# Down-projection by seven block products for nine pairs of feature tiles, in a one-core decoder block

## The chip, the cores and the metric

One core of a Trainium2 chip runs the whole kernel. The metric is device time in microseconds (us). Before the change three runs took 1463.87 us in the median (1459.05 to 1466.71). The engines are TensorE (PE, with its weight loads as PEld), VectorE (DVE), ScalarE (ACT), GpSimd (POOL) and SyncE (SP, which here issues the DMAs).

## The reference, cut to what matters

```python
# L = 1040 positions (16 meta tokens + 1024), D_MODEL = 1024, D_FF = 2816, float32
def _conv_ffn(xn, w_up, conv_w, conv_b, w_down):
    h = xn @ w_up                                      # L x 1024 times 1024 x 5632
    hp = jnp.pad(h, ((0, 0), (CONV_WIDTH - 1, 0), (0, 0)))
    hc = conv_b + sum(conv_w[k] * hp[:, k:k + L] for k in range(CONV_WIDTH))
    gate, up = jnp.split(hc, 2, axis=-1)
    return (jax.nn.silu(gate) * up) @ w_down           # the down-projection: L x 2816 times 2816 x 1024

def reference(...):
    h = concat(meta_tokens, x)
    h = h + _token_mixer(_rmsnorm(h, g_attn), ...)     # two kinds of attention, one output projection
    h = h + _conv_ffn(_rmsnorm(h, g_ffn), ...)
    return _rmsnorm(h, g_final)[:, N_META:]
```

## The kernel before, in words

The kernel runs through attention, the output projection, the up-projection with convolution and gate (the "up phase"), and the down-projection with the last norm (the "down phase"). Every float32 product is made of three matmuls on float32r parts: a matrix is split into a high part (an ACT cast, L856) and a low part (a subtraction, L857, on POOL), and high x high, high x low and low x high are summed in PSUM.

**Up phase (the loop over `ff` from `PLAIN` = 3 to 21, matmuls at L1012).** The 2816 features are 22 tiles of 128. For each feature tile the gate and the up weights (`raw` tiles, two buffers) come in by DMA; POOL makes four sums of their halves (L990 to L993, in `load_up`); four weight entries are split into `dh`/`dl` (three buffers), and seven products of half size give gate and up for both halves of the tokens. These are already Winograd's seven products, on tokens by model dimension. `rest()` ends a tile: `gate` (L1020 to L1024) applies SiLU, multiplies gate and up (L1022) and writes 256 KB of gated features into the DRAM tensor `gated`. `rest()` of one tile is called after the first product of the next tile. The first three feature tiles are done by `plain_chunk`, ahead of this loop. The tokens' own parts `yh`/`yl` and their sums `s1`, `s2`, `s4` stay in SBUF through the phase.

**Down phase (L1077 on).** `load_down` brings in the gated rows of one feature tile (`hr`, 128 features x 1024 tokens) and its rows of `w_down` (`raw`, 128 x 1024), and splits both (L856 on ACT, L857 on POOL, 1024 columns each). Feature tiles go in groups of two, then five times four. For each group, each of eight token tiles and each of two column halves, one PSUM bank takes 3 matmuls of 128x128 by 128x512 per feature tile (L1115), and DVE adds the bank to the residual in SBUF (L1116). In the last group the last norm follows each token tile and its rows go out.

**What sets the order.** The source gives data flow. The framework orders each engine's instructions, DMA issues included, at build time by a simulated timeline, with program order as priority, and an instruction that the simulation finds ready may be put ahead of earlier ones. On the chip each engine then works strictly in that order. All the DMAs here go through SP's one queue. A tile waits until the last reader of what lay at its place is done (`reuse_waits="tile"`). The tiles of the down phase's pool `ph` lie where `yh`, `yl` and, above these, the pool of `s1`, `s2`, `s4` lay.

Of the kernel before, what the change touches and what calls it, by code (L numbers as in the profile page):

```python
# [8 lines left out]
F32 = mybir.dt.float32  # L9
F32R = mybir.dt.float32r  # L10
BF16 = mybir.dt.bfloat16
I32 = mybir.dt.int32
AF = mybir.ActivationFunctionType
ALU = mybir.AluOpType
# [3 lines left out]
P = 128  # L18
D = 1024
SEQ = 1024  # L20
META = 16
L = SEQ + META
KT = D // P
NT = SEQ // P
# [12 lines left out]
HALF = SEQ // 2  # L37
SUB = HALF // 2
PLAIN = 3
G_DOWN = 4  # L40
SLOTS = 9
B_EARLY = 0
TL = True
A_BUFS = 7
# [19 lines left out]
def f(ap):  # L64
    return ap.bitcast(F32)
# [25 lines left out]
def hybrid_block(ctx: ExitStack, tc: tile.TileContext, x, meta, g_attn, w_in, lq1, lk1, lq2, lk2,  # L91
# [49 lines left out]
    def rstd(pool, ss, n, tag):  # L141

        w = pool.tile([P, 4], F32, tag=tag, name=tag, bufs=4)
        l, y, m, u = (w[:n, i : i + 1] for i in range(4))
        nc.scalar.activation(l, ss, AF.Ln, bias=eps[:n], scale=1.0 / D)
        nc.scalar.activation(y, l, AF.Exp, scale=-0.5)
        nc.vector.tensor_scalar(m, ss, 1.0 / D, EPS, op0=ALU.mult, op1=ALU.add)
        nc.vector.tensor_scalar(u, m, y, y, op0=ALU.mult, op1=ALU.mult)
        nc.vector.tensor_scalar(u, u, -0.5, 1.5, op0=ALU.mult, op1=ALU.add)
        nc.vector.tensor_scalar(m, u, y, None, op0=ALU.mult)  # L150
        return m
# [34 lines left out]

    merged = dram.tile([UNITS, P, 2, NQ], F32, name="merged")
    y_rows = dram.tile([NT + 1, P, D], F32, name="y_rows")
    gated = dram.tile([NF, P, SEQ], F32, name="gated")

    left, left_out, right, right_a, right_b = (ExitStack() for _ in range(5))
    pw = ctx.enter_context(tc.tile_pool(name="pw", bufs=1, side="left"))
# [455 lines left out]
    def load_raw(src):  # L648
        raw = pw.tile([P, D], F32, tag="raw", name="raw", bufs=2)
        nc.sync.dma_start(raw, src)  # L650
        return raw
# [13 lines left out]
    def resid(t):  # L665
        return room["accm"][:2] if t == 0 else room["acc"][:, t - 1, :]
# [158 lines left out]


    right_f, right_g, left_s = ExitStack(), ExitStack(), ExitStack()
    pf = right_f.enter_context(tc.tile_pool(name="pf", bufs=1, side="right", reuse_waits="tile"))

    yh = [pf.tile([P, KT, HALF + 2], F32R, name=f"yh{h}") for h in range(2)]  # L830
    yl = [pf.tile([P, KT, HALF + 2], F32R, name=f"yl{h}") for h in range(2)]
    pd = right_f.enter_context(tc.tile_pool(name="pd", bufs=1, side="right", reuse_waits="tile"))
    pg = right_g.enter_context(tc.tile_pool(name="pg", bufs=1, side="right", reuse_waits="tile"))
    gb = pg.tile([P, D], F32, tag="gb", name="g_ffn_b")
    nc.sync.dma_start(gb, g_ffn.broadcast_to([P, D]))
# [16 lines left out]
    def split_w(pool, tags, src, bufs):  # L852
        hi = pool.tile([P, D], F32R, tag=tags[0], name=tags[0], bufs=bufs)
        lo = pool.tile([P, D], F32R, tag=tags[1], name=tags[1], bufs=bufs)
        w = src.shape[-1]
        nc.scalar.copy(hi[:, :w], src)  # L856
        nc.gpsimd.tensor_tensor(lo[:, :w], src, f(hi)[:, :w], op=ALU.subtract)  # L857
        return hi, lo

    def conv(c, src, fc):  # L860

        n = c.shape[-1]
        taps = [src[:, j : j + n] if len(src.shape) == 2 else src[:, :, j : j + n] for j in range(3)]
        nc.scalar.activation(c, taps[2], AF.Identity, bias=cb[:, fc : fc + 1], scale=cw[:, fc, 2:3])
        for j in (1, 0):
            nc.vector.scalar_tensor_tensor(c, taps[j], cw[:, fc, j : j + 1], c, op0=ALU.mult, op1=ALU.add)  # L866
# [132 lines left out]
    def prepare(k):  # L999
        if k < len(entries):  # L1000
            ff, i = entries[k]
            if i == 0:
                load_up(ff)
            ready[k] = split_w(pd, ("dh", "dl"), raws[ff][i], 3)
# [15 lines left out]
    def gate(ff, cg, cu, h):  # L1020
        silu = nc.scalar.activation(cg[:, h], cg[:, h], AF.Silu)
        nc.vector.tensor_tensor(cg[:, h], cg[:, h], cu[:, h], op=ALU.mult)  # L1022
        nc.sync.dma_start(gated[ff, :, HALF * h : HALF * h + HALF], cg[:, h].rearrange("p s c -> p (s c)"))
        return silu  # L1024

    prepare(0)
    prepare(1)
    rest = None
    for ff in range(PLAIN, NF):
        k = 4 * (ff - PLAIN)  # L1030
        cg = pw.tile([P, 2, 2, SUB], F32, tag="wh", name="cg", bufs=2)
        cu = pw.tile([P, 2, 2, SUB], F32, tag="wl", name="cu", bufs=2)
        prepare(k + 2)
        w = ready.pop(k)
        x, y = pair(), pair()
        product(x, w, 0, a11, True, False)
        p1, copied = kept(x, pn, "mc", 2)
        if rest:
            with tc.issue_after(copied.ins):
                rest()  # L1040
        product(y, w, HD, a12, True, True)
        nc.vector.tensor_tensor(y, p1, y, op=ALU.add)
        prepare(k + 3)
        w = ready.pop(k + 1)
        z = pair()
        product(x, w, 0, s2, False, False)
        u2, copied = kept(x, pn, "mc", 2)
        with tc.issue_after(copied.ins):
            conv(cg[:, 0], y, ff)
        product(z, w, HD, s3, True, False)  # L1050
        p7, _ = kept(z, pn, "yb", 1)
        prepare(k + 4)
        w = ready.pop(k + 2)
        product(x, w, 0, s1, False, True)
        u4, copied = kept(x, pn, "mc", 2)
        nc.vector.tensor_tensor(x, p7, x, op=ALU.add)
        product(z, w, HD, a22, False, True)
        nc.vector.tensor_tensor(z, u2, z, op=ALU.add)
        conv(cu[:, 1], x, NF + ff)
        conv(cg[:, 1], z, ff)  # L1060
        prepare(k + 5)
        w = ready.pop(k + 3)
        v = pair()
        product(v, w, 0, s4, True, True)
        nc.vector.tensor_tensor(v, u4, v, op=ALU.add)

        def rest(ff=ff, cg=cg, cu=cu, v=v):
            last = gate(ff, cg, cu, 1)
            conv(cu[:, 0], v, NF + ff)
            return last, gate(ff, cg, cu, 0)  # L1070
    silus = rest()
    banks.close()
    left_s.close()
    right_f.close()
# [1 line left out]

    psd = banks.enter_context(tc.tile_pool(name="psd", bufs=1, space=PSUM, reuse_waits="tile"))  # L1077
    ph = ctx.enter_context(tc.tile_pool(name="ph", bufs=1, side="right", reuse_waits="tile"))
    slot = [0]

    def load_down(ff):
        k = slot[0] % SLOTS
        slot[0] += 1
        hr = pw.tile([P, D], F32, tag="wh", name="hr", bufs=2)
        nc.sync.dma_start(hr, gated[ff])
        got = []
        for what, src in (("h", hr), ("w", load_raw(w_down[P * ff : P * (ff + 1), :]))):
            got.append(split_w(ph, (f"{what}h{k}", f"{what}l{k}"), src, 1))
        return got

    groups, ff = [], 0
    for n in [2] * (NF % G_DOWN // 2) + [G_DOWN] * (NF // G_DOWN):
        groups.append(range(ff, ff + n))
        ff += n
    assert ff == NF
    loaded = {0: [load_down(ff) for ff in groups[0]]}
    with tc.issue_after(silus[0].ins), tc.issue_after(silus[1].ins):
        nc.scalar.preload_act_table_set("natural_log_exp_and_others")
    for gi, group in enumerate(groups):
        last = gi == len(groups) - 1  # L1100
        if last:
            gb = pw.tile([P, D], F32, tag="wl", name="g_final_b", bufs=2)
            nc.sync.dma_start(gb, g_final.broadcast_to([P, D]))
        else:
            loaded[gi + 1] = [load_down(ff) for ff in groups[gi + 1]]
        pairs = loaded.pop(gi)
        for t in range(1, NT + 1):
            h = resid(t)
            tsl = slice(P * (t - 1), P * t)
            for half in range(2):  # L1110
                hs = slice(512 * half, 512 * half + 512)
                ps = psd.tile([P, 512], F32, tag="d", name="ps_d", bufs=8)
                for j, ((gh, gl), (wh, wl)) in enumerate(pairs):
                    for i, (a, b) in enumerate(((gh, wh), (gh, wl), (gl, wh))):
                        nc.tensor.matmul(ps, a[:, tsl], b[:, hs], start=(j == 0 and i == 0), stop=(j == len(pairs) - 1 and i == 2))  # L1115
                nc.vector.tensor_tensor(h[:, hs], h[:, hs], ps, op=ALU.add)  # L1116
            if last:
                ss = pn.tile([P, 1], F32, tag="ssf", name="ssf", bufs=4)
                yn = pw.tile([P, D], F32, tag="wh", name="yn", bufs=2)
                nc.scalar.activation(yn, h, AF.Square, accum_out=ss)  # L1120
                r = rstd(pn, ss, P, "rf")
                for half in range(2):
                    hs = slice(512 * half, 512 * half + 512)
                    nc.vector.scalar_tensor_tensor(h[:, hs], h[:, hs], r, gb[:, hs], op0=ALU.mult, op1=ALU.mult)
                    nc.sync.dma_start(out[P * (t - 1) : P * t, hs], h[:, hs])


# [39 lines left out]
```

## Time and profile before

| | before |
|---|---|
| median of 3 runs | 1463.87 us |
| profiled execution | 1460.51 us, its span 1458.8 us |
| mean granted TensorE clock | 0.979 |
| PE busy | 1379.6 us (95%) |
| DVE / ACT / POOL busy | 854.9 / 687.4 / 679.5 us |
| up phase, L1012, from the chain | 849.99 to 1199.55 us |
| down phase, L1115, from the chain | 1211.06 to 1450.97 us |

The profile is one execution. Its span runs from the first to the last instruction; 1.7 us of the execution's time lie around it. Busy time of an engine is not progress: an instruction that waits inside the engine counts as busy. The chain of waits goes back from the last instruction to whatever released it, so it tells which engine set the end at each time.

### The profile page before, as it was taken

The page shows a single profiled execution, that of the slowest core. Times are in us where ns is not written, and L with a number is a line of the kernel's source. Part 1 is how long each engine was busy: PE and PEld are TensorE (multiplying, and loading weights), DVE is VectorE, ACT ScalarE, POOL GpSimd, SP SyncE. Part 2 cuts the span into 40 slices and gives each one's busy share as a digit, 9 for nine tenths or more (in the row PEclk, how much of TensorE's full clock was granted, in tenths as well). Part 3 has the DMA queues.
Part 4 walks back from the last instruction along what each step waited for, and adds up shares of the span by engine and source line. Part 5 has one row for each costly group of instructions (what it writes and reads, how often), then busy time and mean ns, then how long its engine had stood idle before and what let it go on. Part 6 is the DMA issues. An engine that isn't in the chain of part 4 may idle for free.

```text
span 1458.8 us, 24218 instructions
## 1 busy us (share of the span) xinstructions
PE 1379.6 (95%) x9108; PEld 1275.5 (87%) x9108; DVE 854.9 (59%) x1705; ACT 687.4 (47%) x1379; POOL 679.5 (47%) x706
## 2 busy tenths in 40 slices
PE   5999999998999979898999899999999998999997
PEld 5999999998888877676799899999999997888886
DVE  8377777767676748865777445444454445222235
ACT  6355655665665746433444344444445445212102
POOL 5112222257585655742003466766667649555300
PEclk9999999999999989899999999999999999999999
DMA  5112212212111145345443222222222236433002
GB/s 210 51 33 62 66 52 66 62 47 68 44 51 39 36 123 142 90 96 115 119 158 130 64 84 87 66 80 74 87 85 69 80 102 214 132 115 116 29 15 101
DMA packets 71532, 126.20 MB, mean 87 GB/s; under 512 B 9180, under 2 KB 43612, under 8 KB 71416
## 3 DMA queue, kind: packets, MB, share of 16 engines
q1 hardware_dynamic: 71416, 124.66, 28.0%
q8 instruction: 72, 1.18, 0.3%
q14 instruction: 44, 0.36, 0.1%
HBM read 87.89 MB, written 28.34 MB: 80 GB/s over the span
## 4 chain that ended last, share of the span: by engine, by line
PE 80%; DVE 9%; DMA 4%; ACT 2%; issue 2%; POOL 2%; SPq 0%; DVEq 0%; POOLq 0%; ACTq 0%
PE x L1012 26%; PE ps_d L1115 16%; PE ps_mm L273 15%; PE ps_mm L709 5%; PE ps_av L568 4%; PE ps_tr L540 4%; DVE s L477 2%; PE ps_s L420 2%; PE ps_s L421 2%; DMA mt<-merged 2%; PE ps_s L876 2%; PE ps_av L876 2%; PE ps_tr L174 1%; DMA rd<-y_rows 1%; DMA raw<-in_w_in 1%
## 5 line engine op out<-in xcount | busy, mean ns | idle before, releaser
L273 PE MATMUL ps_mm<-xT_hi,wh 128*128 128x342 f32 (+7 forms) x552 | 186.0, 338 | 5.1 <-DVE qz L283 2.7
L273 PE MATMUL ps_mm<-xT_lo,wh 128*128 128x342 f32 (+7 forms) x552 | 179.9, 326 | 0.2 <-DVE xT_lo L178 0.2
L273 PE MATMUL ps_mm<-xT_hi,wl 128*128 128x342 f32 (+7 forms) x552 | 178.9, 325 | 0.0
L1116 DVE TENSOR_TENSOR acc<-acc,ps_d 128x512 f32<-128x512 f32 x96 | 65.4, 687 | 146.7 <-PE ps_d L1115 146.7
L1115 PE MATMUL ps_d<-wh,hh 128*128 128x512 f32 x352 | 136.7, 392 | 4.7 <-DVE cu L866 3.7
L568 PE MATMUL ps_av<-aT,v 128*128 128x256 f32 (+3 forms) x608 | 121.8, 298 | 16.8 <-DVE aT L553 8.9
L1115 PE MATMUL ps_d<-wl,hh 128*128 128x512 f32 x352 | 137.3, 390 | 0.0
L1115 PE MATMUL ps_d<-wh,hl 128*128 128x512 f32 x352 | 136.5, 390 | 0.0
L857 POOL TENSOR_TENSOR dl<-raw,dh 128x1024 fp32r<-128x1024 f32 (+1 forms) x43 | 82.1, 1910 | 103.1 <-ACT dh L856 103.1
L1012 PE MATMUL x<-yh,dh 128*128 128x258 f32 x608 | 124.3, 286 | 0.0
L1012 PE MATMUL x<-yl,dh 128*128 128x258 f32 x608 | 124.1, 285 | 0.0
L1012 PE MATMUL x<-yh,dl 128*128 128x258 f32 x608 | 123.9, 285 | 0.0
L568 PEld LDWEIGHTS ps_av<-aT,v 128*128 128x128 f32 (+2 forms) x608 | 95.7, 192 | 29.9 <-DVE aT L553 11.4
L477 DVE TENSOR_TENSOR_SCAN s<-s 128x912 f32<-128x912 f32 (+6 forms) x72 | 100.1, 1395 | 23.5 <-POOL s L473 19.5
L273 PEld LDWEIGHTS ps_mm<-xT_hi,wh 128*128 128x128 f32 x552 | 105.4, 191 | 8.3 <-issue 3.1
L1018 ACT COPY kept<-x 128x516 f32<-128x516 f32 x76 | 44.7, 588 | 136.3 <-PE x L1012 136.3
L273 PEld LDWEIGHTS ps_mm<-xT_lo,wh 128*128 128x128 f32 x552 | 105.3, 191 | 0.9 <-DVE xT_lo L178 0.5
L273 PEld LDWEIGHTS ps_mm<-xT_hi,wl 128*128 128x128 f32 x552 | 105.1, 190 | 0.4
L478 POOL TENSOR_TENSOR a<-a,s 128x912 f32<-128x912 f32 (+3 forms) x64 | 83.7, 1309 | 36.1 <-DVE s L477 20.6
L552 ACT CAST aT<-ps_tr 128x512 fp32r<-128x512 f32 (+3 forms) x132 | 66.8, 508 | 62.8 <-PE ps_tr L540 60.2
L553 DVE TENSOR_TENSOR aT<-ps_tr,aT 128x512 fp32r<-128x512 f32 (+3 forms) x132 | 76.8, 586 | 33.3 <-ACT aT L552 32.0
L1012 PEld LDWEIGHTS x<-yl,dh 128*128 128x128 f32 x608 | 95.6, 192 | 0.0
(263 smaller groups left out, 3818.5 us busy)
## 6 DMA issues: line engine op xcount, KB each, us to landing
raw<-in_w_up SPq DMA_DIRECT2D x44, 512.0 KB, 4.0
raw<-in_w_in SPq DMA_DIRECT2D x24, 512.0 KB, 3.9
raw<-in_w_down SPq DMA_DIRECT2D x22, 512.0 KB, 4.2
hr<-gated SPq DMA_DIRECT2D x22, 512.0 KB, 4.0
gated<-cg SPq DMA_DIRECT2D x38, 256.0 KB, 4.1
qs<-qz SPq DMA_DIRECT2D x48, 128.0 KB, 2.7
merged<-mc SPq DMA_DIRECT2D x24, 256.0 KB, 4.2
mt<-merged SPq DMA_DIRECT2D x32, 192.0 KB, 4.2
```

The source lines that it names most:

```text
L273: nc.tensor.matmul(ps[:, :w], a[:, kt * P : (kt + 1) * P], b[:, kt, c0 : c0 + w], start=(kt == 0 and i == 0), stop=(kt == KT - 1 and i == 2))
L477: nc.vector.tensor_tensor_scan(s[:n, rev], s[:n, rev], s[:n, rev], 1.0, op0=ALU.mult, op1=ALU.bypass)
L478: (nc.gpsimd if t else nc.vector).tensor_tensor(b[:n, :keys], b[:n, :keys], s[:n, 1 : keys + 1], op=ALU.mult)
L540: pe_last[0] = nc.tensor.transpose(ps[:kn, at : at + qn], a[:qn, kk0 : kk0 + kn], ident[:qn, :qn])
L552: nc.scalar.copy(aT[:kn, 0, f0:end], ps[:kn, f0:end])
L553: nc.vector.tensor_tensor(aT[:kn, 1, f0:end], ps[:kn, f0:end], f(aT)[:kn, 0, f0:end], op=ALU.subtract)
L568: pe_last[0] = nc.tensor.matmul(av[:, :w], v[:kn, kt, vi, :], aT[:kn, ai, j * w : (j + 1) * w], start=count == 0, stop=count == n_todo - 1)
L709: nc.tensor.matmul(ps[:n], a, b[:, hs], start=(j == 0 and i == 0), stop=(j == len(wo) - 1 and i == 2))
L857: nc.gpsimd.tensor_tensor(lo[:, :w], src, f(hi)[:, :w], op=ALU.subtract)
L1012: nc.tensor.matmul(x[:, s], w[a][:, ks], y[b][:, kt, SUB * s : SUB * s + SUB + 2], start=start and kt == 0 and i == 0, stop=kt == KT // 2 ...
L1115: nc.tensor.matmul(ps, a[:, tsl], b[:, hs], start=(j == 0 and i == 0), stop=(j == len(pairs) - 1 and i == 2))
L1116: nc.vector.tensor_tensor(h[:, hs], h[:, hs], ps, op=ALU.add)
```

## The change

In the down phase, feature tiles 4 to 21 are taken in nine pairs. For a pair, the gated features form a matrix of 2 x 2 blocks (two halves of 512 tokens by two feature tiles), and the rows of `w_down` one of 2 x 2 blocks (two feature tiles by two halves of 512 columns). Seven block products replace eight. Each block product is 4 token tiles x 3 matmuls of 128x512, so a pair has 84 matmuls in place of 96. Feature tiles 0 to 3 (`N_ROWS`) stay as they were, as a last group of four.

- The seven left operands of a pair are seven blocks of 128 x 512 in a new DRAM tensor `blocks`. Three of them are gated features as they are; four are sums, made on DVE in the up phase by `gated_sums`, four subtractions or additions of 128 x 512 per pair, called one feature tile later. A third buffer for `cg` is added for it.
- The seven right operands are made from the two `w_down` tiles by four DVE operations per pair, in `take`.
- An "entry" is one left and one right block, split together into one high and one low tile: two ACT casts of 128 x 512; the right block's low part on POOL, the left block's low part on DVE for odd entries and on POOL for even ones. Twelve entries are made ahead: three in `dh`/`dl`, which now live through the down phase, and nine in `ph`. Left blocks are loaded into eight buffers `a`.
- Pairs go in groups of three. In a group, seven "chains" each add three block products to four PSUM banks, and DVE adds the banks to a quarter of the residual after each chain. Banks `x` go on accumulating over several chains, by Winograd's sums.
- The `w_down` tiles of a pair are a "set"; five sets are in flight, in the `raw`, `wh` and `wl` buffers and four tiles of `ph`.
- The pool `pd` is now opened ahead of `pf`, so `dh`/`dl` and `yh`/`yl` change places.

```diff
-    gated = dram.tile([NF, P, SEQ], F32, name="gated")
+    gated = dram.tile([N_ROWS, P, SEQ], F32, name="gated")
+    blocks = dram.tile([N_PAIRS, 7, P, HALF], F32, name="blocks")
...
         nc.vector.tensor_tensor(cg[:, h], cg[:, h], cu[:, h], op=ALU.mult)
-        nc.sync.dma_start(gated[ff, :, HALF * h : HALF * h + HALF], cg[:, h].rearrange("p s c -> p (s c)"))
+        if ff < N_ROWS:
+            nc.sync.dma_start(gated[ff, :, HALF * h : HALF * h + HALF], flat(cg[:, h]))
+        elif ((ff - N_ROWS) % 2, h) in BLOCKS:
+            put_block(ff, BLOCKS[(ff - N_ROWS) % 2, h], cg[:, h])
...
+    def gated_sums(ff, before, cg, cu):
+        (a11, a21), (a12, a22) = ([flat(t[:, h]) for h in range(2)] for t in (before, cg))
+        s3, s1 = (flat(cu[:, h]) for h in range(2))
+        nc.vector.tensor_tensor(s3, a11, a21, op=ALU.subtract)
+        put_block(ff, 3, cu[:, 0])
+        nc.vector.tensor_tensor(s1, a21, a22, op=ALU.add)
+        put_block(ff, 4, cu[:, 1])
+        nc.vector.tensor_tensor(a11, s1, a11, op=ALU.subtract)
+        put_block(ff, 2, before[:, 0])
+        nc.vector.tensor_tensor(a12, a12, a11, op=ALU.subtract)
+        put_block(ff, 6, cg[:, 0])
...
-        cg = pw.tile([P, 2, 2, SUB], F32, tag="wh", name="cg", bufs=2)
+        pool, tag, bufs = (pw, "wh", 2) if ff % 3 else (ps_, "cg", 1)
+        cg = pool.tile([P, 2, 2, SUB], F32, tag=tag, name="cg", bufs=bufs)
...
         conv(cg[:, 1], z, ff)
+        if sums_of:
+            gated_sums(*sums_of)
+            sums_of = None
         prepare(k + 5)
...
+    def take(k):
+        i, q = steps[k]
+        pool, tags, bufs = (pd, ("dh", "dl"), 3) if k % ENTRIES < 3 else (ph, ("eh", "el"), ENTRIES - 3)
+        hi, lo = (pool.tile([P, D], F32R, tag=tag, name=tag, bufs=bufs) for tag in tags)
+        taken[k] = hi, lo
+        if q >= N_PAIRS:                               # the four plain feature tiles
...
+        a = ph.tile([P, HD], F32, tag="a", name="a", bufs=8)
+        nc.sync.dma_start(a, blocks[q, i])
...
+        for src, cs, engine in ((a, lower, nc.vector if k % 2 else nc.gpsimd), (b, upper, nc.gpsimd)):
+            nc.scalar.copy(hi[:, cs], src)
+            engine.tensor_tensor(lo[:, cs], src, f(hi)[:, cs], op=ALU.subtract)
+        if i == 0:                                     # three sums of w_down blocks; one more at i == 1
...
+        if i == 6 and q + SETS < N_PAIRS + N_ROWS:
+            load_set(q + SETS)
...
+    CHAINS = (("x", True, 0, lower), ("y", True, 0, lower), ("x", False, half_nt, lower), ("y", True, half_nt, upper),
+              ("x", False, half_nt, upper), ("y", False, half_nt, lower), ("x", False, 0, upper))
+    for q in range(SETS):
+        load_set(q)
+    for k in range(ENTRIES):
+        take(k)
...
+    for group in groups:                               # three groups of three pairs
+        for tag, begin, rows, cs in CHAINS:
...
+            for t in range(half_nt):
+                for j in range(len(group)):
+                    hi, lo = taken[k + j]
+                    for i, (a, b) in enumerate(((hi, hi), (hi, lo), (lo, hi))):
+                        nc.tensor.matmul(ps, a[:, tsl], b[:, upper], start=begin and j == 0 and i == 0, ...)
+                add(1 + t + rows, cs, ps)
+            for _ in group:
+                take(k + ENTRIES)
+                k += 1
```

## Rows read from the trace of the kernel before

**Rows 1.** The page's busy time: us (share of the span) and instructions by engine.
```profile
span 1458.8 us, 24218 instructions
...
PE 1379.6 (95%) x9108; PEld 1275.5 (87%) x9108; DVE 854.9 (59%) x1705; ACT 687.4 (47%) x1379; POOL 679.5 (47%) x706
```
**Rows 2.** Chain that ended last from 850 us: start, us, what (xN: instructions).
```profile
849.99 349.56 PE x L1012 x2887
...
1211.06 239.91 PE ps_d L1115 x1051
```
**Rows 3.** Busy us of each engine in two stretches, then PEclk, DMA share, GB/s.
```profile
1100.00:1200.00 100.00, 100.00 (x829) 100.00 (x828) 49.15 (x69) 48.09 (x70) 62.23 (x37) 1.00 0.27 86
...
1300.00:1400.00 100.00, 100.00 (x442) 82.82 (x442) 25.43 (x37) 14.09 (x14) 33.11 (x14) 1.00 0.16 53
```
**Rows 4.** Instructions from 1211 us by line and shape: busy us, mean ns, idle before.
```profile
L1116 DVE TENSOR_TENSOR acc<-acc,ps_d 128x512 f32<-128x512 f32 x96 | 65.4, 687 | 146.7 <-PE ps_d L1115 146.7
L857 POOL TENSOR_TENSOR wl<-raw,wh 128x1024 fp32r<-128x1024 f32 x21 | 50.9, 2429 | 0.9 <-ACT wh L856 0.9
```
**Rows 5.** Timeline of PE, end of the up phase: start us, us, line, operation [idle before].
```profile
1202.04 0.41 PE L1012 MATMUL x<-yh,dl 128*128 128x258 f32 x2
...
1204.47 0.41 PE L1012 MATMUL x<-s4h,dl 128*128 128x258 f32 x2
...
1205.93 1.43 PE L1115 MATMUL ps_d<-wh,hh 128*128 128x512 f32 x5 [1.05 <-ACT wh L856]
...
1211.06 1.62 PE L1115 MATMUL ps_d<-wh,hh 128*128 128x512 f32 x3 [3.70 <-DVE cu L866]
```
**Rows 6.** Timeline of DVE and POOL in the same stretch.
```profile
1207.35 5.12 POOL L857 TENSOR_TENSOR wl<-raw,wh 128x1024 fp32r<-128x1024 f32 x2
...
1208.20 2.05 DVE L1022 TENSOR_TENSOR cg<-cg,cu 128x512 f32<-128x512 f32 x1
...
1210.94 2.07 DVE L1022 TENSOR_TENSOR cg<-cg,cu 128x512 f32<-128x512 f32 x1
...
1212.43 2.83 POOL L857 TENSOR_TENSOR hl<-hr,hh 128x1024 fp32r<-128x1024 f32 x1
```
**Rows 7.** Timeline of the last up iteration: a cast on ACT, and POOL.
```profile
1177.11 1.32 POOL L991 TENSOR_TENSOR tb<-raw 128x512 f32<-128x512 f32 x1
1178.37 1.31 POOL L992 TENSOR_TENSOR tb<-raw,ta 128x512 f32<-128x512 f32 x1
1179.63 2.41 POOL L857 TENSOR_TENSOR dl<-raw,dh 128x1024 fp32r<-128x1024 f32 x1
...
1185.93 2.41 POOL L857 TENSOR_TENSOR dl<-ta,dh 128x1024 fp32r<-128x1024 f32 x1
...
1190.15 0.62 ACT L856 CAST dh<-raw 128x512 fp32r<-128x512 f32 x1 [0.35 <-ACT cg L1021]
...
1190.85 1.29 POOL L857 TENSOR_TENSOR dl<-raw,dh 128x512 fp32r<-128x512 f32 x1 [2.52 <-ACT dh L856]
```
**Rows 8.** Timeline of the same iteration: PE's first product, an SP load, DVE.
```profile
1171.84 0.33 SPq L650 DMA_DIRECT2D raw<-in_w_up  x1
...
1184.35 0.41 PE L1012 MATMUL x<-yh,dh 128*128 128x258 f32 x2
...
1188.65 0.69 DVE L1022 TENSOR_TENSOR cg<-cg,cu 128x512 f32<-128x512 f32 x1 [2.44 <-ACT cg L1021]
...
1191.82 0.88 DVE L1022 TENSOR_TENSOR cg<-cg,cu 128x512 f32<-128x512 f32 x1
1194.87 1.54 DVE L866 SCALAR_TENSOR_TENSOR cg<-x,cw,cg 128x512 f32<-128x512 f32 x2 [2.18 <-ACT cg L864]
1200.24 0.70 DVE L1056 TENSOR_TENSOR x<-kept,x 128x516 f32<-128x516 f32 x1 [3.84 <-ACT kept L1018]
```
**Rows 9.** DMA issues: KB each, median us to landing.
```profile
gated<-cg SPq DMA_DIRECT2D x38, 256.0 KB, 4.1
...
rd<-y_rows SPq DMA_DIRECT2D x8, 256.0 KB, 3.7
```

More of the change, by code (lines that the diff above doesn't have):

```diff
@@ L39 @@
 PLAIN = 3
-G_DOWN = 4
-SLOTS = 9
+N_ROWS = 4
+N_PAIRS = (NF - N_ROWS) // 2
+G_PAIRS = 3
+ENTRIES = 12
+SETS = 5
 B_EARLY = 0
@@ L827, in hybrid_block @@
     right_f, right_g, left_s = ExitStack(), ExitStack(), ExitStack()
+    pd = ctx.enter_context(tc.tile_pool(name="pd", bufs=1, side="right", reuse_waits="tile"))
     pf = right_f.enter_context(tc.tile_pool(name="pf", bufs=1, side="right", reuse_waits="tile"))
-    yh = [pf.tile([P, KT, HALF + 2], F32R, name=f"yh{h}") for h in range(2)]
-    yl = [pf.tile([P, KT, HALF + 2], F32R, name=f"yl{h}") for h in range(2)]
-    pd = right_f.enter_context(tc.tile_pool(name="pd", bufs=1, side="right", reuse_waits="tile"))
+    yh, yl = ([pf.tile([P, KT, HALF + 2], F32R, name=f"y{h}{p}") for h in range(2)] for p in "hl")
     pg = right_g.enter_context(tc.tile_pool(name="pg", bufs=1, side="right", reuse_waits="tile"))
@@ L1022, in gate, with flat, put_block @@
         nc.vector.tensor_tensor(cg[:, h], cg[:, h], cu[:, h], op=ALU.mult)
-        nc.sync.dma_start(gated[ff, :, HALF * h : HALF * h + HALF], cg[:, h].rearrange("p s c -> p (s c)"))
-        return silu
+        if ff < N_ROWS:
+            nc.sync.dma_start(gated[ff, :, HALF * h : HALF * h + HALF], flat(cg[:, h]))
+        elif ((ff - N_ROWS) % 2, h) in BLOCKS:
+            put_block(ff, BLOCKS[(ff - N_ROWS) % 2, h], cg[:, h])
+        return silu
+    BLOCKS = {(0, 0): 0, (1, 0): 1, (1, 1): 5}
+    def flat(v):
+        return v.rearrange("p s c -> p (s c)")
+    def put_block(ff, i, src):
+        nc.sync.dma_start(blocks[(ff - N_ROWS) // 2, i], flat(src))
+    def gated_sums(ff, before, cg, cu):
[9 more added lines that the diff above has]
+        put_block(ff, 6, cg[:, 0])
     prepare(0)
     prepare(1)
-    rest = None
+    rest = sums_of = before = None
     for ff in range(PLAIN, NF):
         k = 4 * (ff - PLAIN)
-        cg = pw.tile([P, 2, 2, SUB], F32, tag="wh", name="cg", bufs=2)
+        pool, tag, bufs = (pw, "wh", 2) if ff % 3 else (ps_, "cg", 1)
+        cg = pool.tile([P, 2, 2, SUB], F32, tag=tag, name="cg", bufs=bufs)
         cu = pw.tile([P, 2, 2, SUB], F32, tag="wl", name="cu", bufs=2)
@@ L1070, in rest @@
             return last, gate(ff, cg, cu, 0)
+        if ff >= N_ROWS and (ff - N_ROWS) % 2:
+            sums_of = ff, before, cg, cu
+        before = cg
     silus = rest()
+    gated_sums(*sums_of)
     banks.close()
@@ L1078, in hybrid_block @@
     ph = ctx.enter_context(tc.tile_pool(name="ph", bufs=1, side="right", reuse_waits="tile"))
[L1079 to L1096, printed above, removed]
+    lower, upper = slice(0, HD), slice(HD, D)
+    groups = [range(p, min(p + G_PAIRS, N_PAIRS)) for p in range(0, N_PAIRS, G_PAIRS)]
+    steps = [(i, p) for group in groups for i in range(7) for p in group]
+    n_blocks = len(steps)
+    steps += [(i, N_PAIRS + r) for r in range(N_ROWS) for i in range(2)]
@@ new lines, in hybrid_block, with load_set @@
+    sets, taken = {}, {}
+    def load_set(q):
+        pool, tags, bufs = ((pw, ("raw",) * 2, 2), (ph, ("r0", "r1"), 1), (ph, ("r2", "r3"), 1),
+                            (pw, ("wh",) * 2, 2), (pw, ("wl",) * 2, 2))[q % SETS]
+        got = [pool.tile([P, D], F32, tag=tag, name="wd", bufs=bufs) for tag in tags]
+        if q < N_PAIRS:
+            ff = N_ROWS + 2 * q
+            srcs = [w_down[P * r : P * (r + 1), :] for r in (ff, ff + 1)]
+        else:
+            ff = q - N_PAIRS
+            srcs = [gated[ff], w_down[P * ff : P * (ff + 1), :]]
+        for dst, src in zip(got, srcs):
+            nc.sync.dma_start(dst, src)
+        sets[q] = got
@@ new lines, in take @@
+    def take(k):
+        if k >= len(steps):
+            return
+        i, q = steps[k]
[3 more added lines that the diff above has]
+        if q >= N_PAIRS:
+            src = sets[q][i]
+            nc.scalar.copy(hi, src)
+            for engine, cs in ((nc.gpsimd, lower), (nc.vector, upper)):
+                engine.tensor_tensor(lo[:, cs], src[:, cs], f(hi)[:, cs], op=ALU.subtract)
+            return
+        a = ph.tile([P, HD], F32, tag="a", name="a", bufs=8)
+        nc.sync.dma_start(a, blocks[q, i])
+        r0, r1 = sets[q][:2]
+        b = {0: r0[:, lower], 1: r1[:, lower], 2: sets[q][-1], 3: r0[:, upper], 4: r0[:, lower], 5: r1[:, lower], 6: r1[:, upper]}[i]
+        for src, cs, engine in ((a, lower, nc.vector if k % 2 else nc.gpsimd), (b, upper, nc.gpsimd)):
+            nc.scalar.copy(hi[:, cs], src)
+            engine.tensor_tensor(lo[:, cs], src, f(hi)[:, cs], op=ALU.subtract)
+        if i == 0:
+            t2 = ph.tile([P, HD], F32, tag="t2", name="t2", bufs=SETS)
+            sets[q].append(t2)
+            nc.vector.tensor_tensor(r0[:, lower], r0[:, upper], r0[:, lower], op=ALU.subtract)
+            nc.vector.tensor_tensor(t2, r1[:, upper], r0[:, lower], op=ALU.subtract)
+            nc.vector.tensor_tensor(r0[:, upper], r1[:, upper], r0[:, upper], op=ALU.subtract)
+        if i == 1:
+            nc.vector.tensor_tensor(r1[:, lower], r1[:, lower], sets[q][2], op=ALU.subtract)
+        if i == 6 and q + SETS < N_PAIRS + N_ROWS:
+            load_set(q + SETS)
@@ new lines, in bank_of, with add @@
+    def bank_of(tag):
+        return psd.tile([P, 512], F32, tag=tag, name=f"ps_{tag}", bufs=4)
+    def add(t, cs, ps):
+        h = resid(t)
+        nc.vector.tensor_tensor(h[:, cs], h[:, cs], ps, op=ALU.add)
+    half_nt = NT // 2
+    CHAINS = (("x", True, 0, lower), ("y", True, 0, lower), ("x", False, half_nt, lower), ("y", True, half_nt, upper),
+              ("x", False, half_nt, upper), ("y", False, half_nt, lower), ("x", False, 0, upper))
+    for q in range(SETS):
+        load_set(q)
@@ L1097, in hybrid_block @@
+    for k in range(ENTRIES):
+        take(k)
     with tc.issue_after(silus[0].ins), tc.issue_after(silus[1].ins):
         nc.scalar.preload_act_table_set("natural_log_exp_and_others")
[L1099 to L1125, printed above, removed]
@@ new lines, in hybrid_block @@
+    k = 0
+    for group in groups:
+        chains = {}
+        for tag, begin, rows, cs in CHAINS:
+            if begin:
+                chains[tag] = [bank_of(tag) for _ in range(half_nt)]
+            for t in range(half_nt):
+                ps = chains[tag][t]
+                tsl = slice(P * t, P * (t + 1))
+                for j in range(len(group)):
+                    hi, lo = taken[k + j]
+                    for i, (a, b) in enumerate(((hi, hi), (hi, lo), (lo, hi))):
+                        nc.tensor.matmul(ps, a[:, tsl], b[:, upper], start=begin and j == 0 and i == 0,
+                                         stop=j == len(group) - 1 and i == 2, skip_group_check=True)
+                add(1 + t + rows, cs, ps)
+            for _ in group:
+                del taken[k]
+                take(k + ENTRIES)
+                k += 1
@@ new lines, in hybrid_block @@
+    gb = pw.tile([P, D], F32, tag="wh", name="g_final_b", bufs=2)
+    nc.sync.dma_start(gb, g_final.broadcast_to([P, D]))
+    rows = [(*taken[k + 2 * r], *taken[k + 2 * r + 1]) for r in range(N_ROWS)]
+    for t in range(1, NT + 1):
+        h = resid(t)
+        tsl = slice(P * (t - 1), P * t)
+        for cs, tag in ((lower, "y"), (upper, "x")):
+            ps = bank_of(tag)
+            for j, (gh, gl, wh, wl) in enumerate(rows):
+                for i, (a, b) in enumerate(((gh, wh), (gh, wl), (gl, wh))):
+                    nc.tensor.matmul(ps, a[:, tsl], b[:, cs], start=(j == 0 and i == 0), stop=(j == N_ROWS - 1 and i == 2))
+            add(t, cs, ps)
+        ss = pn.tile([P, 1], F32, tag="ssf", name="ssf", bufs=4)
+        junk = pn.tile([P, D], BF16, tag="yb", name="junk")
+        nc.scalar.activation(junk, h, AF.Square, accum_out=ss)
+        r = rstd(pn, ss, P, "rf")
+        for cs in (lower, upper):
+            nc.vector.scalar_tensor_tensor(h[:, cs], h[:, cs], r, gb[:, cs], op0=ALU.mult, op1=ALU.mult)
+            nc.sync.dma_start(out[P * (t - 1) : P * t, cs], h[:, cs])
```

## The prediction

> **What bounds the kernel now.** I read busy time first: PE is busy for 1379.6 of 1458.8 us, and no other engine for over 59% [rows 1]. That alone does not say that PE sets the end of each stage, so the chain of waits comes second: from 850 us on it is almost only PE, 349.56 us in one piece for the up phase and 239.91 us in one piece for the down phase [rows 2]. Third, the table by stretches: inside both phases PE has no idle time at a granted clock of 1.00, 829 matmuls of 258 columns in 100 us in the up phase and 442 of 512 columns in the down phase [rows 3]. So in the down phase a matmul costs 100 / 442 = 0.2262 us, and one removed there is worth just that as long as its operands still come in time. The only holes are at the passage between the phases [rows 5], so fourth I read this passage and the last up iteration instruction by instruction [rows 5 to 8].
>
> **Removed: matmuls.** Before, 22 feature tiles x 16 banks x 3 = 1056. After, 9 pairs x 7 products x 12 = 756, and 4 feature tiles x 16 x 3 = 192: 948. The shape stays 128x128 by 128x512. 108 x 0.2262 = **24.4 us less**. One block product ("step") takes PE 12 x 0.2262 = 2.71 us.
>
> **Added: adds from PSUM.** 28 per group of three pairs, three groups, and 16 at the end are 100 in place of 96, at 0.69 us [rows 4]. They lie beside PE: a bank is needed again at the earliest one chain (8.1 us) after its add was due, less 2.0 at the passage from one group to the next. Cost 0, while DVE's queue is under 5 us late.
>
> **Moved: the splits, and who does them.** Before, a feature tile with 48 matmuls (10.9 us) had two subtractions of 1024 columns on POOL, 2.43 us each [rows 4]. After, a step of 2.71 us has 1.5 of 512 columns on POOL on average. A POOL operation of 512 columns takes 1.3 us, and the next begins 1.26 us after it [rows 7]: 1.89 us per step. DVE gets 31 subtractions for odd entries and 9 x 4 sums of weights, 67 operations in 63 steps, each with both inputs in SBUF. Such an operation takes 0.69 us when POOL is idle [rows 8], but 2.05 and 2.07 us when POOL is at work, and the POOL operation that starts during one takes 2.83 us in place of 2.43 [rows 4, 6]. I read this as taking turns: DVE waits until POOL's operation ends, and POOL then loses some 0.4 to 0.45 us. POOL per step: 1.89 + 67/63 x 0.45 = 2.37 us, under PE's 2.71. The Trainium skill ("SBUF — State Buffer", section Who interferes with whom) says that a DVE instruction with two SBUF inputs and a GpSimd instruction that reads SBUF exclude each other, and that the second one blocks for the whole of the first. The rows agree on the waiting; the blocked POOL operation here lost 0.4 and not the full 0.69 us. By the rule the step would cost POOL 1.89 + 0.73 = 2.62 us, still under PE's, but with nothing in hand.
>
> DVE per group (21 steps, 57.0 us): 28 adds are 19.3 us, 22.3 operations with two SBUF inputs are 0.69 us each plus a wait between 0 and 1.3 us (a whole POOL operation of 512). At 0.65 us that is 49 us, at 1.3 us it is 63.7. I take the middle, since POOL is at work some 70% of the time and an operation arrives anywhere in it; then PE stays the bound and the cost is 0. The upper end is 3 x 6.7 = 20 us. ACT has two casts of 0.62 us [rows 7] per step, far below 2.71. DMA per pair is seven blocks of 256 KB and 1 MB of weights in 19 us, 147 GB/s; the nearest row of such a read lands in 3.7 us [rows 9], and eight buffers are loaded ahead: 0.
>
> **Moved: the passage to the down phase.** Before, the last up matmul ends at 1204.9 and the chain's PE part at 1451.0 [rows 2, 5]: 246.1 us for 1056 matmuls, 238.9 at full pace, so 7.2 us are lost in it: 1.05 waiting for ACT, 3.70 for a PSUM bank that the convolution's last step frees, 2.4 in slower pace and short waits behind these. After, the first chain needs three entries. Their weights can be there early. Their left blocks cannot: buffers `a` lie, by the order of allocation, where the second half's `yh` lay, and its last reader ends near 1202.4 [rows 5]. A load of 256 KB then lands 3.7 us after its issue [rows 9], at about 1206.3, its cast ends at 1206.9, and PE starts 2.0 us after the up phase's end. The PSUM banks of the first chain are then free. Entries 3 to 8 need 9 POOL operations; DVE has 2 gate products, 4 sums of the last pair, 9 sums of weights and 3 subtractions at this time, so POOL pays about 1.26 + 0.45 us for each: entries 0 to 2 by 1209.5, 3 to 5 by 1216.3, 6 to 8 by 1224.9, against PE's wish at 1215.0 and 1224.4. That is 2.0 + 1.3 + 0.5 us, 2.4 for the pace behind the gap as before, and I add 2 for DVE's order in a full queue: 8 us, **1 us more** than before. Ends: 2 us lost (5 less than now), or 15 more if SP's queue stands (below).
>
> **Added in the up phase.** 36 sums on DVE, 27 DMA writes of 256 KB more (63 blocks and 2 rows against 38 [rows 9]), and a buffer. PE sees them only through what they delay. DVE is half idle there [rows 3]; four sums are 2.8 us each second iteration, and in an iteration DVE has holes of 2.18 and 3.84 us, the first of them just behind the gate products that the sums need, while POOL has nothing from 1192.1 on [rows 7, 8]. The nearest deadline is POOL's: the second weight load is issued at 1171.84, its sums and the split for the next tile end at 1182.0, and PE takes it at 1184.2 [rows 7, 8], so 2.2 us of slack. A write of 256 KB takes 4.1 us with others under way [rows 9], and queued ahead of that load it could eat half of the slack. I take **1 us**; ends are 0 and the slower case below. That `pd` and `pf` change places touches tiles that are freed by the end of attention: 0.
>
> **The sum.** On the profiled execution: 1460.51 - 24.4 + 1 + 1 = 1438.1 us. The tail from 1451.0 on is the same in both. That execution is 3.4 us under the median of runs, so a median could lie at 1441.5; I forecast **1440 us**, with 1433 to 1447 for this case.
>
> **Rivals.**
> - *DVE and POOL pace the down phase.* For: 67 operations that take turns with POOL, DVE waiting for up to 1.3 us each; past a mean wait of 1.0 us DVE needs more than 57.0 us per group. Against: at 0.65 us it has 8 us per group to spare. With 1.15 us it is 3.3 us per group, 10 in all: 1450; at the end of its range 1460.
> - *The first loads stand behind the last buffers.* Sets 3 and 4 go into the last `cg` and `cu`, which are free only when the last sums have been written: about 1213.6 for DVE and 4 more for the write. If the order in SP's queue puts them ahead of the left blocks, the first chain starts near 1222 and not 1207: 15 us more, 1455. For: one queue for all loads. Against: the order comes from a simulated timeline, which should see these buffers as late; before, the loads of the last group were put where their buffers came free.
> - *The sums hold up the up phase: slower.* If the four sums are placed where the source has them, behind the convolution, they meet POOL's splits of 2.41 us [rows 7], and each can wait out one: 8 us. If then their DMA writes stand ahead of the next weight load in SP's queue, this load is 8 us late, 6 past its slack, nine times: 54 us, 1492. It decides the sign from 2.2 + 22.4 / 9 = 4.7 us of delay per pair. Against: the hole behind the gate products is earlier, POOL is idle in it, and the load's condition comes before the sums'.
> - *The passage improves.* Only the 2.0 us are lost: 1435. It is inside the likeliest's range.
>
> **How the numbers follow.** Likeliest, passage improved included, 0.70; paced by DVE and POOL 0.13; SP's queue at the passage 0.08; slower through the up phase 0.06; 0.03 for what I have not seen. A median of this kernel can be told from no change from about 0.5%, 7.3 us: the borders are 1456.5 and 1471.2. The first two cases and most of the third are faster: 0.87. Within the borders lie the upper ends of the second and third, and a delay of 4 to 6 us per pair: 0.07. Slower: 0.06. The range leaves out the slower case and the worst of pacing: 1432 to 1455.
>
> **What would show it.** Right: 948 matmuls at L1115's successor, 0.226 us apart, PE without holes after the first chains; POOL near 85% and DVE near 80% busy in the down phase; DVE operations with two SBUF inputs at 0.7 to 2 us; up iterations still 20.3 us apart. Wrong: PE idle inside a chain, released by POOL or DVE (pacing); SP waiting for the last block writes with the left blocks behind it; L990 starting later than 4.1 us after POOL's last split in every second iteration.

## The result and the profile after

The changed kernel is slower by 0.6%: 1471.59 us in the median of 7 runs (1465.03 to 1477.11), against 1462.31 us for the kernel before in its 7 runs; the ratio is 1.0059, interval [1.0034, 1.0084]. The forecast was 1440 us, 1432 to 1455.

The page of the changed kernel, busy time in us as in [rows 1]:

```profile
span 1469.6 us, 24501 instructions
...
PE 1361.1 (93%) x9000; PEld 1258.2 (86%) x9000; DVE 971.6 (66%) x1820; ACT 718.4 (49%) x1469; POOL 737.1 (50%) x765
```

108 matmuls are gone, 9108 to 9000, as forecast, and yet the span is 10.8 us longer. The chain that ended last, from 817 us, as in [rows 2] (start, us, what):

```profile
817.03 385.83 PE x L1015 x3173
...
1209.97 2.07 DMA blocks<-cg
...
1216.46 8.05 DMA a<-blocks
...
1248.64 0.61 DVE acc L1176
1249.39 8.92 PE ps_x L1201 x28
...
1272.40 0.69 DVE acc L1176
1273.09 1.75 DVE wd L1163
...
1385.56 8.16 PE ps_y L1201 x36
...
1459.00 2.73 PE ps_x L1218 x12
```

Before, the down phase was one piece of PE. Now it begins with a DMA of left blocks, goes through pieces of DVE, and only from some 1361 us to the last matmul is it PE alone, 36 matmuls in 8.16 us: 0.2267 us each, the pace that the prediction had. The stretches of the down phase (busy us of PE, PEld, DVE, ACT, POOL; PEclk, DMA share, GB/s), as in [rows 3]:

```profile
1212.00:1225.00 13.00, 0.00 (x0) 0.00 (x0) 1.99 (x3) 1.08 (x2) 1.26 (x1) 0.50 0.95 349
1225.00:1249.00 24.00, 19.05 (x72) 15.21 (x72) 21.60 (x14) 14.61 (x28) 23.77 (x15) 0.86 0.39 132
...
1272.00:1299.00 27.00, 20.76 (x92) 16.87 (x90) 26.56 (x23) 9.77 (x18) 27.00 (x17) 0.93 0.31 108
...
1361.00:1418.00 57.00, 57.00 (x252) 47.18 (x252) 33.53 (x44) 18.13 (x28) 37.89 (x26) 1.00 0.23 74
```

Two losses stand apart: PE does nothing while the DMA engines run at 0.95 and 349 GB/s (the passage), and PE has holes where POOL and DVE are both busy nearly all the time (the heads of the groups of pairs).

**The account.** I measure the down phase from the end of the last up matmul to the end of the last matmul, less the matmuls at 0.2262 us each. Before: 246.1 - 238.9 = 7.2 us lost. After: 1461.72 - 1205.15 = 256.57, less 948 x 0.2262 = 214.44, is 42.1 us lost. That is 34.9 us more; 24.4 us of matmuls were saved; the up phase took 388.2 us (817.0 to 1205.2) against 389.3; and what lies ahead of it took 1.4 us more: 34.9 - 24.4 - 1.1 + 1.4 = 10.8. Of the 42.1 us PE stands idle for 33 (20.1 in the passage, 12.9 in three waits for DVE's adds). The other 9 are matmuls at a slower pace behind these waits, where the granted clock is below 1.00: 0.86 and 0.93 in the stretches above, after 0.50 while PE did nothing.

PE's own waits in the passage and at the first chain (timeline of PE, start, us, operation [idle before <-releaser]):

```profile
1225.20 0.79 PE L1201 MATMUL ps_x<-dh 128*128 128x512 f32 x1 [20.06 <-ACT dh L1158]
1249.39 0.76 PE L1201 MATMUL ps_x<-eh 128*128 128x512 f32 x1 [5.14 <-DVE acc L1176]
```

The wait of 20.06 us answers to the 1.05 and 3.70 us of [rows 5]. ACT, the releaser named, was itself waiting for the DMA of the first left block. Why so late is seen in SP's queue (timeline of SP):

```profile
1211.42 0.32 SPq L1039 DMA_DIRECT2D blocks<-cg  x1
1212.79 0.33 SPq L1136 DMA_DIRECT2D wd<-in_w_down  x1
1213.21 0.38 SPq L1039 DMA_DIRECT2D blocks<-cg  x1
1213.69 2.73 SPq L1136 DMA_DIRECT2D wd<-in_w_down  x5
1216.46 0.92 SPq L1154 DMA_DIRECT2D a<-blocks  x2
```

The left blocks (`a`) are issued behind the last block write of the up phase, at 1213.21, and behind five loads of 512 KB, and land 8.05 us later.

The second loss, in the timelines of DVE and POOL in the first stretch after the start:

```profile
1238.43 1.78 DVE L1164 TENSOR_TENSOR t<-wd 128x512 f32<-128x512 f32 x1
1240.13 1.78 DVE L1165 TENSOR_TENSOR wd<-wd 128x512 f32<-128x512 f32 x1
1241.84 1.78 DVE L1167 TENSOR_TENSOR wd<-wd,t 128x512 f32<-128x512 f32 x1
...
1248.57 2.47 DVE L1176 TENSOR_TENSOR acc<-acc,ps_x 128x512 f32<-128x512 f32 x4
```

```profile
1237.92 1.74 POOL L1159 TENSOR_TENSOR el<-a,eh 128x512 fp32r<-128x512 f32 x1
1239.62 1.74 POOL L1159 TENSOR_TENSOR el<-t,eh 128x512 fp32r<-128x512 f32 x1
1241.32 1.75 POOL L1159 TENSOR_TENSOR el<-a,eh 128x512 fp32r<-128x512 f32 x1
```

Both engines advance in steps of 1.70 us: one POOL operation (1.26 us apart when nothing stands in the way) and one DVE operation with two SBUF inputs per step. POOL loses some 0.45 us, as foreseen from [rows 6]. A DVE operation, 0.69 us by itself, holds DVE's queue for 1.70 us. The first four adds from PSUM banks come at 1248.57, behind twelve such operations in a row (1228.24 to 1248.65), and PE waits for them.

### The profile page after: what moved, and what is told of

Read it like the earlier page. It is cut to its first block, busy times and chain, and to the rows that moved or that the text cites. A ratio compares the mean times of both kernels' runs of the same rounds, so it can differ in the third digit from the quotient of the medians.

```text
span 1469.6 us, 24501 instructions
## 1 busy us (share of the span) xinstructions
PE 1361.1 (93%) x9000; PEld 1258.2 (86%) x9000; DVE 971.6 (66%) x1820; ACT 718.4 (49%) x1469; POOL 737.1 (50%) x765
## 4 chain that ended last, share of the span: by engine, by line
PE 73%; DVE 12%; DMA 5%; issue 4%; POOL 2%; ACT 2%; SPq 1%; DVEq 0%; POOLq 0%; ACTq 0%
PE x L1015 26%; PE ps_mm L277 15%; PE ps_x L1201 5%; PE ps_av L572 4%; PE ps_mm L713 4%; PE ps_tr L544 3%; PE ps_y L1201 3%; DVE s L481 2%; DMA mt<-merged 2%; PE ps_s L424 2%; PE ps_s L425 2%; PE ps_s L879 2%; PE ps_av L879 2%; PE ps_x L1218 1%; PE ps_y L1218 1%
## 5 line engine op out<-in xcount | busy, mean ns | idle before, releaser
L482 POOL TENSOR_TENSOR a<-a,s 128x912 f32<-128x912 f32 (+3 forms) x64 | 84.2, 1317 | 36.6 <-DVE s L481 20.4
L544 PE MATMUL ps_tr<-ident,a 128*128 128x128 f32 (+1 forms) x540 | 91.4, 276 | 2.9 <-DVE v L341 1.7
L258 POOL TENSOR_TENSOR wl<-raw,wh 128x1024 fp32r<-128x1024 f32 x25 | 61.9, 2480 | 57.8 <-ACT wh L257 55.2
L424 PE MATMUL ps_s<-kz,qz 128*128 128x456 f32 (+9 forms) x240 | 81.4, 344 | 1.2 <-ACT a L470 1.0
L869 DVE SCALAR_TENSOR_TENSOR cg<-x,cw,cg 128x512 f32<-128x512 f32 x76 | 56.9, 749 | 35.7 <-ACT cg L867 35.0
L1159 POOL TENSOR_TENSOR el<-wd,eh 128x512 fp32r<-128x512 f32 x39 | 59.3, 1533 | 34.8 <-ACT eh L1158 21.9
L425 PE MATMUL ps_s<-kz,qs 128*128 128x456 f32 (+9 forms) x240 | 74.7, 315 | 0.0
L544 PEld LDWEIGHTS ps_tr<-ident,a 128*128 128x128 f32 (+1 forms) x540 | 60.6, 132 | 11.9 <-DVE v L341 2.4
L869 DVE SCALAR_TENSOR_TENSOR cu<-x,cw,cu 128x512 f32<-128x512 f32 x76 | 56.8, 748 | 16.4 <-ACT cu L867 16.3
```

What stands on the lines that cost most here:

```text
L424: nc.tensor.matmul(ps[:n, :wide], qz[:, m, c : c + n], kz[:, m, c0 : c0 + wide], start=True, stop=False)
L425: pe_last[0] = nc.tensor.matmul(ps[:n, :wide], qs[:, m, c - cq : c - cq + n], kz[:, m, c0 : c0 + wide], start=False, stop=True)
L482: (nc.gpsimd if t else nc.vector).tensor_tensor(b[:n, :keys], b[:n, :keys], s[:n, 1 : keys + 1], op=ALU.mult)
L544: pe_last[0] = nc.tensor.transpose(ps[:kn, at : at + qn], a[:qn, kk0 : kk0 + kn], ident[:qn, :qn])
```

## Experiments

All are compared with the kernel before on the same chip. Its own median differs from set to set: 1462.3 us beside the changed kernel, 1461.3 beside e1, e2, e3 and e12, 1463.3 beside the rest. So a difference of two medians from different sets is uncertain by 1 to 2 us beyond the noise; the ratios are not. Medians in us; the last two columns are from each one's profile: matmul time lost in the down phase, by the account above, and the longest wait of PE in it.

| kernel | median | ratio to before, interval | lost | longest wait |
|---|---|---|---|---|
| after | 1471.6 | 1.0059 [1.0034, 1.0084] | 42.1 | 20.1 |
| e1, third buffer's place | 1459.9 | 0.9989 [0.9967, 1.0011] | 29.4 | 9.0 |
| e2, pair splits on DVE | 1455.6 | 0.9951 [0.9932, 0.9970] | 23.7 | 20.4 |
| e3, no weight sums | 1453.2 | 0.9938 [0.9916, 0.9961] | 23.1 | 20.2 |
| e12, e1 and e2 | 1439.2 | 0.9856 [0.9819, 0.9892] | 9.3 | 4.6 |
| e1s, e1 and later sums | 1460.5 | 0.9979 [0.9958, 0.9999] | 30.5 | 11.9 |
| e4, e1 and pair splits on POOL | 1460.0 | 0.9986 [0.9968, 1.0004] | 30.2 | 13.8 |
| e12s, e12 and later sums | 1440.3 | 0.9854 [0.9833, 0.9875] | 9.4 | 5.4 |
| e12 again | 1437.9 | 0.9846 [0.9820, 0.9871] | 9.4 | 4.6 |

### The place of the third buffer (e1)

The tiles of the down phase reuse the place of the pool `ps_`, in which the change had put the third `cg` buffer. That buffer held the last feature tile (21 is a multiple of 3), and its last reader is the very last block write. One row of the changed kernel (timeline of ACT) shows the place at work: the first cast into a tile `eh` of the down phase waits for that write, which was issued at 1213.21.

```profile
1217.60 0.62 ACT L1158 CAST eh<-wd 128x512 fp32r<-128x512 f32 x1 [9.09 <-DMA blocks<-cg]
```

```diff
-        pool, tag, bufs = (pw, "wh", 2) if ff % 3 else (ps_, "cg", 1)
+        pool, tag, bufs = (pw, "wh", 2) if ff % 3 != 1 else (ps_, "cg", 1)
```

> Edit: the third cg buffer serves feature tiles 4, 7, ... 19 and no longer 3, 6, ... 21, so the last tile's cg is in the wh buffers. Queue theory (S): the down phase's pool comes into use only when all that lay at its place is read, and the last reader was the last block write out of that third buffer; so the left blocks stood behind it in SP's queue. With the edit the first chain starts near 1209 us and not 1225: 1471.6 - 14 = 1457. Rival N (the slow chains that follow come only from the late start, since no lead was built): these go as well, 1437. Rival to S (the left blocks wait for the matmuls' end or for the weight loads, not for the third buffer): no change, 1471.

1459.9 us, 11.7 less than after (10.2 by the ratios). SP's queue and PE's first waits in the down phase of this kernel:

```profile
1198.96 8.77 SPq L1136 DMA_DIRECT2D wd<-in_w_down  x5
1207.77 5.44 SPq L1154 DMA_DIRECT2D a<-blocks  x7
1215.59 0.92 SPq L1039 DMA_DIRECT2D blocks<-cg  x2
```

```profile
1215.69 0.79 PE L1201 MATMUL ps_x<-dh 128*128 128x512 f32 x1 [4.96 <-ACT dh L1158]
...
1241.82 0.47 PE L1201 MATMUL ps_x<-eh 128*128 128x512 f32 x1 [4.87 <-DVE acc L1176]
...
1293.50 0.77 PE L1201 MATMUL ps_x<-eh 128*128 128x512 f32 x1 [9.00 <-DVE acc L1176]
```

The left blocks now go out ahead of the last block writes, and the passage costs 4.96 us of idle PE instead of 20.06. The queue theory holds in that the third buffer's last reader set the start; the trace shows no addresses, so whether the left blocks' own buffers lay at its place, or were only ordered behind it in the queue, is not shown. The rival on the late start falls: the waits for DVE's adds are still there, 15.1 us in three. The median gained 11.7 and not 14; these waits grew, from 12.9 us.

### All pair splits on DVE (e2)

```diff
-        for src, cs, engine in ((a, lower, nc.vector if k % 2 else nc.gpsimd), (b, upper, nc.gpsimd)):
+        for src, cs, engine in ((a, lower, nc.vector), (b, upper, nc.vector)):
```

> Edit: both low parts of every pair entry are made on DVE, none on POOL. Lock theory (L): a DVE operation with two SBUF inputs takes 1.7 us only because it takes turns with POOL's; without POOL it is 0.6, a step needs some 2.35 us of DVE against 2.71 of PE, and the slow chains at the heads of the groups lose most of their 21 us: 1453 to 1458. Rival W (DVE has too much work in the down phase, whoever else works): 94 more operations of 0.6 us on the same engine make it worse, 1485 or more. Rival N (late start): no change, 1471.

1455.6 us, 16.0 less, with 95 splits more (the expectation says 94) on the engine that was late. The same stretches as above in e2:

```profile
1225.00:1249.00 24.00, 24.00 (x97) 19.57 (x96) 24.00 (x41) 16.76 (x33) 0.00 (x0) 0.90 0.73 217
...
1272.00:1299.00 27.00, 27.00 (x121) 22.37 (x120) 23.52 (x40) 8.25 (x15) 0.00 (x0) 1.00 0.27 79
```

The durations of one kind of split and of one kind of sum on DVE in e2 (ns, least/median/most), then of the same sum in the changed kernel:

```profile
L1159 DVE TENSOR_TENSOR el<-a,eh x45: 683/695/739, 1228.9 to 1360.9; 128x512 fp32r<-128x512 f32 x45
...
L1163 DVE TENSOR_TENSOR wd<-wd x9: 685/693/718, 1196.2 to 1323.9; 128x512 f32<-128x512 f32 x9
```

```profile
L1163 DVE TENSOR_TENSOR wd<-wd x9: 678/1760/1782, 1198.3 to 1346.8; 128x512 f32<-128x512 f32 x9
```

In the changed kernel the sums of L1163 had a median of 1760 ns; in e2 none is over 718. DVE does 41 operations in 24 us where it did 14, and PE has no hole after the start. Rival W, too much work for DVE, is out: it was the turns with POOL.

### Without the sums of weights (e3)

The four `tensor_tensor` lines of `take` at `i == 0` and `i == 1` are left out.

> Edit: the four sums of weight blocks per pair are left out (the products then use the plain weight blocks, so the output is not the reference's); the rest stays. If it is the burst of sums at a group's head, 1.7 us each ahead of the adds in DVE's queue, that holds PE: 36 operations fewer, 10 to 15 us faster, 1457 to 1461, and the gaps at the second and third group's heads vanish. If the takings of turns with the splits hold PE by themselves: at most 5 us, 1466. Rival N: no change, 1471.

1453.2 us, 18.4 less, a little past the forecast. PE's only wait in the down phase is the passage (total us, times, longest):

```profile
PE ps_x L1195 <- ACT dh L1158: 20.2, 1, 20.2
```

The 31 splits on DVE still take turns with POOL, for up to 1.82 us each, but these turns alone do not hold PE. It takes the sums as well: 36 operations of up to 1.78 us in one queue with the adds.

### Both edits (e12)

> Edit: the third buffer's place and all pair splits on DVE, the two together. S and L add up: 1471.6 - 14 - 17 = 1440, range 1435 to 1446, faster than both kernels. If W holds: slower than the third buffer's edit alone. If N holds: equal to the third buffer's edit alone.

1439.2 us, and 1437.9 in the second set. PE waits 4.64 us at the passage and 0.55 us once more (timeline of PE), and is the chain from 1237 us on:

```profile
1208.84 0.79 PE L1201 MATMUL ps_x<-dh 128*128 128x512 f32 x1 [4.64 <-ACT dh L1158]
1237.29 0.50 PE L1201 MATMUL ps_y<-eh 128*128 128x512 f32 x1 [0.55 <-DVE acc L1176]
```

In matmul time lost the two gains add up: 12.7 + 18.4 = 31.1, measured 32.8. In the medians they are 11.7 + 16.0 = 27.7 against 32.4; the interval of e12 is some 5 us to either side. This is the time that was forecast for the change, within 1 to 2 us, and it is 1.5% under the kernel before.

### Later sums (e1s and e12s)

```diff
-        if i == 0:
+        if i == 1:
...
+        if i == 2:
             nc.vector.tensor_tensor(r0[:, upper], r1[:, upper], r0[:, upper], op=ALU.subtract)
-        if i == 1:
+        if i == 3:
```

> Edit on top of the third buffer's: the same four sums of weight blocks per pair, at the latest places instead of the first: two with the pair's second entry, one with its third, one with its fourth (before: three with the first, one with the second). The work stays the same in kind and count, turns with POOL too. If it is the burst that puts DVE late, against a mean rate that fits: the waits for DVE's adds at the group heads fall from 15 us to under 5, 1460 - 10 = 1450. If the mean rate with turns of 1.7 us is too high (22 such operations of 1.7 us and 28 adds of 0.6 us are 54 us per group of 57): 2 us at most, 1458.

> Edit: the third buffer's place, all pair splits on DVE, and the later sums. DVE's queue at the passage is shorter by some 3 operations of 0.6 us: 1439 - 1 = 1438, 1434 to 1442. If the order of the sums there matters more, down to 1434; if DVE's rate were the bound in the whole down phase, no change.

e1s took 1460.5 us, no gain on e1 (ratios 0.9979 and 0.9989, overlapping intervals). The edit did not do what it was meant to: on DVE the sums still stand in a bunch, now between 1266 and 1287 us,

```profile
1276.12 1.78 DVE L1159 TENSOR_TENSOR dl<-a,dh 128x512 fp32r<-128x512 f32 x1
1277.82 1.77 DVE L1164 TENSOR_TENSOR t<-wd 128x512 f32<-128x512 f32 x1
1279.51 1.76 DVE L1166 TENSOR_TENSOR wd<-wd 128x512 f32<-128x512 f32 x1
1281.19 0.68 DVE L1177 TENSOR_TENSOR acc<-acc,ps_y 128x512 f32<-128x512 f32 x1
```

probably because entries are made twelve ahead and the order is the framework's; that was not tested. Whether spread sums would do with the turns in place stays open. On top of e12 the edit changes nothing that can be measured (1440.3 against 1437.9 us, overlapping intervals).

### All pair splits on POOL (e4)

```diff
-        for src, cs, engine in ((a, lower, nc.vector if k % 2 else nc.gpsimd), (b, upper, nc.gpsimd)):
+        for src, cs, engine in ((a, lower, nc.gpsimd), (b, upper, nc.gpsimd)):
```

> Edit on top of the third buffer's: all low parts of the pairs on POOL, so that DVE has only the 36 weight sums and the adds. Lock theory: POOL needs 2 x 1.26 us and 0.45 us for each sum, 2.78 us a step against PE's 2.71, so POOL paces by a little, while DVE is free for the adds: 1450 to 1458, with PE waiting for POOL's low parts and no longer for DVE's adds. If POOL's share of the splits had been the trouble all along: over 1465.

1460.0 us: within 2 us of the upper end, and for another reason than expected. PE did not wait for POOL's low parts (1.1 us in all) but for DVE's adds, 16.5 us in all, 13.79 of them behind one sum (timelines of DVE, POOL and PE):

```profile
1265.96 16.49 DVE L1163 TENSOR_TENSOR wd<-wd 128x512 f32<-128x512 f32 x1 [3.06 <-POOL el L1159]
```

```profile
1265.90 1.27 POOL L1159 TENSOR_TENSOR el<-a,eh 128x512 fp32r<-128x512 f32 x1
1267.14 1.28 POOL L1159 TENSOR_TENSOR el<-wd,eh 128x512 fp32r<-128x512 f32 x1
...
1279.43 2.47 POOL L1159 TENSOR_TENSOR el<-a,eh 128x512 fp32r<-128x512 f32 x2
1283.91 1.60 POOL L1159 TENSOR_TENSOR el<-t,eh 128x512 fp32r<-128x512 f32 x1 [2.01 <-ACT eh L1158]
```

```profile
1285.04 0.79 PE L1201 MATMUL ps_x<-eh 128*128 128x512 f32 x1 [13.79 <-DVE acc L1176]
```

## Why the prediction was wrong

- **Matmuls: right.** 108 fewer, 0.2267 us each where nothing else holds; e12 shows the gain once the rest is out of the way.
- **The up phase: right, and less than taken.** 1 us was taken for the 36 sums and 27 writes; the phase took 388.2 us against 389.3. The slower case through this phase, 0.06, did not come.
- **The passage: wrong.** "A load of 256 KB then lands 3.7 us after its issue, at about 1206.3" took the issue for granted once the place's last matmul was done. The load went out at 1216.46 and landed 8.05 us later, behind five loads of 512 KB. PE stood idle for 20.06 us where the prediction had 2.0. Of the 42.1 us lost, e1 takes away 12.7. The rival that "the first loads stand behind the last buffers" had the place and the price (first chain near 1222, 15 us more), at a chance of 0.08, but not the holder. Loads of sets 3 and 4 did stand ahead of the left blocks, and one of them, at 1212.79, waited 1.0 us for a write out of a `cu` buffer. But e1 changes only which feature tiles use the third `cg` buffer, and with that the left blocks go out ahead of the last block writes: the holder was this buffer, at whose place the new pool has tiles. That the rival's price came out was luck in part. I had read "a third buffer is added" and priced its time, not its address.
- **The splits: wrong in one number, and in taking an average.** "I take the middle", a wait of 0.65 us for each DVE operation with two SBUF inputs, since it arrives anywhere in a POOL operation. It does not: after one turn both wait for each other, and each DVE operation waits for a whole POOL operation. At the heads of the groups that is 1.70 us per operation, a wait of 1.0 us, the point from which the pacing rival decides. The average over a group also hid that the sums come in bunches, ahead of the adds in a queue that keeps its order. So the adds, put at a cost of 0 "while DVE's queue is under 5 us late", held PE for 12.9 us. e2 and e3, each by its own way, take away 18.4 and 19.0 us of the time lost; the rival's worst case was 20.
- **The chances: wrong in kind.** The two rivals were given 0.13 and 0.08 as if each came alone. Both came, and 1438 + 15 + 20 = 1473 was in the text without being added up; measured were 1471.6 us.
- **A slip without weight.** The loads of a pair, 2816 KB in 19 us, are 152 GB/s and not 147.

What stays open: 9.3 us are still lost in e12, 5.2 of them idle and the rest at a lower granted clock behind the gap (0.83 in the 20 us from 1204 us on). The first cast of a left block stands there behind a gate's activation and a table load in ACT's queue, which was not tried otherwise.

## What to carry to other kernels

Work that is moved to an idle engine is to be priced with the engine that it then takes turns with: a DVE operation with two SBUF inputs beside a busy POOL was 1.70 us and not 0.69, and here giving all of it to DVE was faster than sharing it. Ask of each new buffer not only when it is read but what will lie at its place afterwards. Where adds that free PSUM stand in the same queue as work that can block, look at the bunches and not at the average.

## What the runs showed of the hardware that was not expected

A DVE operation with two SBUF inputs does not always get its turn after one POOL operation. In e4, with POOL's queue full, it was held for 16.49 us, over thirteen POOL operations that ran 1.22 to 1.25 us apart and lost nothing, and went through when POOL paused. Right after this pause turns were one to one in e4 too, none over 1.79 us. Two more operations were held for 7.6 and 7.8 us. In the down phase of the changed kernel, with several such operations in DVE's queue one behind the other, turns were one to one, none over 1.79 us. What decides between the two was not found. The Trainium skill ("SBUF — State Buffer", section Summary: rules for kernel authors) says that the second of the two to issue blocks until the first finishes; these runs agree that it blocks, but in e4 it was many operations and not the first alone that had to finish.
